# Both heads of a recurrent unit in one compact 64-wide tile: the triangular inverse, L and W by 64x64 products

## The chip, the cores and the metric

The kernel runs on one core of one Trainium2 chip. The metric is the device time of one execution in microseconds (us); before the change it is 2819.77 us, the median of 3 runs (2819.64 to 2821.25). The trace that is read here comes from one more, profiled execution.

## The reference, cut to what matters

The kernel computes two hybrid decoder layers on 512 tokens of width 1024, in f32. Each layer is a SwiGLU feed-forward, a mixer, and a second feed-forward, each with residual and layer norm. The mixer runs three token mixers beside each other on one projection of the stream and merges them: RWKV-7 (8 heads of width 64), differential attention, and a gated DeltaNet (4 heads of width 128).

RWKV-7 is a recurrence over tokens, per head:

```
S = S * w_t - (S @ kk_t) (kk_t * a_t)^T + v_t k_t^T ;   y_t = S @ r_t
```

The gated DeltaNet is given in chunks of 64 tokens. In both, the kernel works on chunks of 64 tokens. Within a chunk it needs the inverse of I + L, where L is a strictly lower triangular 64x64 matrix:

```
Lm = strict_lower(kb @ k^T * decay) ;  A = Lm + I
U = solve(A, v * beta) ;  W = solve(A, kb * exp(G))
```

512 tokens are 8 chunks, so one head has 8 such 64x64 matrices. The gated DeltaNet in this kernel uses chunks of 128 instead, so 4 matrices of 128x128.

## The kernel before

A feed-forward is a row of wide projections: for each 128 output columns, 24 matmuls of 128x128 against 512 tokens (f32 split into a high and a low f32r part, three products), with the weights streamed by SP's queue through a ring of four buffers. The mixer's projections (`proj`, PSUM tile pj or pgt) are the same, 8 blocks of 3.

The mixer's token mixers are cut into 12 units, `ORDER = RDRDRRDGGDGG`: R is `rw_pair` (one pair of RWKV heads, 4 per layer), D is `da_head`, G is `gdn_head` (4 per layer). Each unit is a Python generator; a yield ends a turn. `main` writes out the projections, and after each piece `interleave` calls `pump`, which gives turns to active units whose last results an estimate (`Estimate`) takes to be ready. At most four units are active. The instructions thus stand in one order written at build time, and the compiler's scheduler may still move independent ones against each other. All matrix work of the units goes through `mm` and `tr`, so the profile shows one line for it, L68; the PSUM tile's name tells products apart: pL, ip (all products of the inverse), pM, pMV, paT, pW, pU (the row name covers pU0 and the per-chunk pU), pb, pk.

One RWKV unit (`rw_pair`), as far as it matters:

- Before L: `be` (128 partitions = 2 heads x 64 channels, 512 tokens) is the vector b of the recurrence, and `AR` holds the a and r sides.
- L: per head and per 128 tokens, one product pL of 64x128 (contraction 64 channels) to a full 128x128 block that holds two chunks; DVE scales each of the 8 blocks by a per-token factor `n2` and by the mask `b_gt`, which is strictly lower triangular and zero between the two chunks. Each head has its own tile L of 128 x (4 blocks x 128).
- `inverse(Ls, whole)`: L goes to DRAM; its 16x16 diagonal blocks come back, one per partition, and DVE inverts them all at once in 15 steps of two operations; they go to DRAM (`Xd`, zero elsewhere) and come back as full 128x128 blocks X. DVE transposes X by 32x32 blocks to Z. Doubling from 16 to 32: per head, four 128x128 products of the masked L (`imL`) with Z, a copy by ACT, four 128x128 products with X, a subtraction and a transpose by DVE. Doubling from 32 to 64: products of 32x32, per head and per chunk position in a PSUM tile of its own (tiles ipt). For the gated DeltaNet (`whole`) one more step, of 64x64.
- Beside the inverse: pk and pb transpose `kap` and `be` to tokens on partitions. For b the second chunk of a 128-token block is wanted on the other half, so the transposes start 64 tokens early, and the first chunk takes a product of its own.
- After the inverse: pM (64x64 products in all four quadrants of the array, with both heads), pMV, then paT (transposes of a), pW, pU0, all of the last with the 128x128 blocks of Z; then eight steps over the chunks (pU, pS) and the output pY.

A matmul of two f32 operands stands in the trace as two records.

Of the kernel before, what the change touches and what calls it, by code (L numbers as in the profile page):

```python
# [9 lines left out]
F32 = mybir.dt.float32  # L10
# [37 lines left out]
BLK = 8 * (16 * 128 + 16)  # L48
# [88 lines left out]
class Net:  # L137
# [47 lines left out]
    def more_consts(self):  # L185
# [22 lines left out]
        def pair(name, src, r0):  # L208
            m = c.tile([P, P], F32, name=name)
            nc.gpsimd.tensor_copy(out=m, in_=src)  # L210
            nc.gpsimd.memset(m[r0:r0 + 64, 64 - r0:128 - r0], 0.0)
            return m

        self.b_gt = pair("b_gt", self.m_gt, 64)

        self.m3 = c.tile([P, 3, 64], F32, name="m3")
        for h in range(2):
            r = slice(64 * h, 64 * h + 64)
            for j in range(3):
# [17 lines left out]
                                fill=0.0, base=2 * b - 1, channel_multiplier=-1)  # L237
        zt = self.t2(name="zt")
        nc.gpsimd.memset(zt, 0.0)
        self.xd, self.nxd = [], 0  # L240
        for _ in range(3):
            t = self.tc.dram_tile([8 * BLK], F32, name="Xd")
            nc.sync.dma_start(out=t[0:128 * 1024].rearrange("(p c) -> p c", p=128)[:, 0:512], in_=zt)
            nc.sync.dma_start(out=t[0:128 * 1024].rearrange("(p c) -> p c", p=128)[:, 512:1024], in_=zt)
            nc.sync.dma_start(out=t[128 * 1024:].rearrange("(p c) -> p c", p=128), in_=zt[:, 0:8])
            self.xd.append(t)
# [558 lines left out]
    def inverse(self, Ls, whole):  # L805
        nc = self.nc
        n = len(Ls)
        r4 = lambda t: t.rearrange("p (n i) -> p n i", n=4)
        blk = lambda t, b: t[:, 128 * b:128 * b + 128]

        Ld = self.tc.dram_tile([8 * BLK], F32, name="Ld")
        Xd = self.xd[self.nxd % len(self.xd)]
        self.nxd += 1
        full = lambda t, e: bass.AP(t.tensor, t.offset + 4 * e * BLK, [[128, 128], [BLK, 4], [1, 128]])
        diag = lambda t: bass.AP(t.tensor, t.offset, [[BLK // 8, 32 * n], [128, 16], [1, 16]])
        B = self.t2((128, 2, 16, 16), name="LX")
        Lb, Xb = B[0:32 * n, 0], B[0:32 * n, 1]
        Tb = self.m128("Tb")[0:32 * n]
# [3 lines left out]
        for e in range(n):  # L822
            nc.sync.dma_start(out=full(Ld, e), in_=r4(Ls[e]))
        nc.sync.dma_start(out=Lb, in_=diag(Ld))
        yield
        mLs = []
        for i in range(15):
            if i % 4 == 3:
                yield
            if i == 7:  # L830
                for L in Ls:
                    mLs.append(self.t2(name="imL"))
                    nc.gpsimd.tensor_tensor(out=r4(mLs[-1]), in0=r4(L), in1=self.bc(self.lev, 4), op=ALU.mult)
            m = 15 - i
            t = Tb[:, 0:m * (i + 1)].rearrange("p (a b) -> p a b", a=m)
            nc.vector.tensor_tensor(out=t, in0=Lb[:, i + 1:16, i:i + 1].to_broadcast([32 * n, m, i + 1]),
                                    in1=Xb[:, i:i + 1, 0:i + 1].to_broadcast([32 * n, m, i + 1]), op=ALU.mult)
# [3 lines left out]
        X = [self.t2(name="iX") for _ in Ls]  # L841
        for e in range(n):
            nc.sync.dma_start(out=r4(X[e]), in_=full(Xd, e))
        yield
        Z = [self.t2(name="iZ") for _ in Ls]
        for e in range(n):
            nc.vector.transpose(out=Z[e], in_=X[e])
        for e in range(n):
# [6 lines left out]
            pz = self.psum(name="ip")  # L855
            for b in range(4):
                self.mm(blk(pz, b), blk(X[e], b), blk(mL, b), start=True, stop=True)
            nc.vector.tensor_tensor(out=Z[e], in0=Z[e], in1=pz, op=ALU.subtract)
            nc.vector.transpose(out=X[e], in_=Z[e])
            yield  # L860

        for w, at in ((32, (0, 64)),) + (((64, (0,)),) if whole else ()):
            pts = []
            for e in range(n):
                L4, Z4 = r4(Ls[e]), r4(Z[e])
                pts.append(self.t2((128, 4, w), name="ipt"))
                for a in at:
                    p = self.psum((128, 4, w), name="ip")
                    for b in range(4):
                        self.mm(p[a:a + w, b, :], L4[a + w:a + 2 * w, b, a:a + w], Z4[a + w:a + 2 * w, b, a + w:a + 2 * w],  # L870
                                start=True, stop=True)
                    nc.scalar.copy(out=pts[e][a:a + w], in_=p[a:a + w])
            yield
            for e in range(n):
                X4, Z4, pt = r4(X[e]), r4(Z[e]), pts[e]
                for a in at:
                    p = self.psum((128, 4, w), name="ip")
                    for b in range(4):
                        self.mm(p[a:a + w, b, :], X4[a:a + w, b, a:a + w], pt[a:a + w, b, :], start=True, stop=True)
                    nc.vector.tensor_scalar(out=Z4[a:a + w, :, a + w:a + 2 * w], in0=p[a:a + w], scalar1=-1.0,  # L880
                                            scalar2=None, op0=ALU.mult)
                if whole and w == 32:
                    p = self.psum((128, 4, w), name="ip")
                    for b in range(4):
                        self.mm(p[w:2 * w, b, :], pt[0:w, b, :], X4[0:w, b, 0:w], start=True, stop=True)
                    nc.scalar.activation(out=X4[w:2 * w, :, 0:w], in_=p[w:2 * w], func=ACTF.Copy, scale=-1.0)
            yield
# [33 lines left out]
    def rw_pair(self, j, r, k, v):  # L921
# [54 lines left out]
        be = t2(name="be")  # L976
        for h in range(2):
            STT(out=hv(be, h), in0=hv(ta, h), scalar=1.0, in1=AR[h][:, :, 0, :], op0=ALU.add, op1=ALU.mult)
        STT(out=be, in0=be, scalar=0.5, in1=G, op0=ALU.mult, op1=ALU.mult)
# [18 lines left out]
        Ls = [t2((128, 4, 128), name="L") for _ in range(2)]  # L998
        ps = [self.psum((128, 4, 128), "pL") for _ in range(2)]
# [9 lines left out]
        inv = self.inverse([L.rearrange("p a b -> p (a b)") for L in Ls], False)  # L1009
# [15 lines left out]
        Z = yield from inv  # L1025

        Ms, Sh = [[], []], []
        for h in range(2):
            ps = [self.psum((128, 2, 3, 64), "pM") for _ in range(2)]
            for tp in range(2):  # L1030
                for q in range(2):
# [3 lines left out]
                    for e in range(2):  # L1035
                        rs = slice(64 * e, 64 * e + 64)
                        self.mm(ps[e][qs, tp, 0:2 + q:1 + q, :], kap[rs, c], AR[h][rs, tp, :, qs], start=True, stop=True)
                        self.mm(ps[e][os, tp, 1 + q, :], be[rs, c], AR[h][rs, tp, 1, qs], start=True, stop=True)
            for e in range(2):
# [4 lines left out]
                Ms[e].append(M)  # L1044
            yield

        nb = nn2[:, :, None].to_broadcast([128, 8, 64])
        R = [t2((128, 4, 2, 64), name="R") for _ in range(2)]
        R8 = [t.rearrange("p t e i -> p (t e) i") for t in R]
# [8 lines left out]
        p = self.psum((128, 4, 128), "paT")  # L1058
        for tt in range(NT):
            self.tr(p[:, tt, :], AR[tt // 2][:, tt % 2, 0, :], self.ident)  # L1060
        TT(out=R8[1], in0=p.rearrange("p t (e i) -> p (t e) i", e=2), in1=nb, op=ALU.mult)

        p = self.psum((128, 4, 128), "pW")
        for tt in range(NT):
            for e in range(2):
                self.mm(p[64 * e:64 * e + 64, tt, :], R[1][:, tt, e, :], Z[e][:, 128 * tt:128 * tt + 128], start=True, stop=True)
        U0, W = (t.rearrange("p t e i -> p t (e i)") for t in R)
        for q in range(2):
            nc.scalar.copy(out=W[:, :, 64 - 64 * q:128 - 64 * q], in_=p[:, :, 64 * q:64 * q + 64])
        p = self.psum((128, 4, 128), "pU0")  # L1070
        for tt in range(NT):
            for e in range(2):
                for q in range(2):
                    c = 2 * tt + q
# [478 lines left out]
```

## Time and profile before

| | |
|---|---|
| median of 3 runs | 2819.77 us |
| the profiled execution | 2822.03 us |
| its span | 2820.3 us |
| mean granted TensorE clock | 0.995 |
| PE busy | 2774.4 us, 98% |
| DVE busy | 1967.5 us, 70% |
| ACT busy | 1111.8 us, 39% |
| POOL busy | 156.7 us, 6% |
| DMA | 282.21 MB, mean 100 GB/s |

The span runs from the first to the last instruction; the time of the execution has a little around it. Busy time is the union of an engine's records. Matmuls are pipelined, and their recorded ends overlap the next one's start; the distance between the starts of two records is what the first of them costs. The granted clock is 1 where TensorE runs at 2.4 GHz and 0.5 where it runs at 1.2 GHz.

The mixing stages lie at about 380 to 1000 us and 1780 to 2400 us; the rest is feed-forward.

### The profile page before, as it was taken

The numbers are of one execution on the slowest core, as the hardware profiler recorded it, in microseconds if no ns is written. First come the engines' busy times: TensorE is split into PE (matmuls) and PEld (weight loads), VectorE is DVE, ScalarE is ACT, GpSimd is POOL, SyncE is SP. The second block draws the span as 40 slices with busy tenths as digits, with TensorE's granted clock in tenths as the row PEclk, the third lists the DMA queues.
The fourth block names the chain that finished last, engine by engine and source line by source line (L and its number), as shares of the span: only waits on it lengthen the run. The fifth ranks groups of instructions, "written<-read, shape, count | busy, mean of one in ns | idle before, by whom it ended". The sixth has DMA issues, their size and how long they took to land. (4 is left out here: it accounts for less than half of the span.)

```text
span 2820.3 us, 40858 instructions
## 1 busy us (share of the span) xinstructions
PE 2774.4 (98%) x15536; PEld 2295.6 (81%) x15536; DVE 1967.5 (70%) x4400; ACT 1111.8 (39%) x2029; POOL 156.7 (6%) x205
## 2 busy tenths in 40 slices
PE   9999999999999999999999999999999999999998
PEld 7888887778888888888888888777788888888887
DVE  6766568788875466667676666677888764666675
ACT  4333345444543333333333333454445433333332
POOL 1000021010000010000100000210100000100001
PEclk9999999999999999999999999999999999999999
DMA  6233523232223353332533324223222223533322
GB/s 212 90 112 99 143 81 80 57 82 56 69 76 85 94 176 116 111 105 87 150 112 107 120 82 137 83 72 77 63 62 69 80 80 106 180 112 107 108 77 89
DMA packets 437381, 282.21 MB, mean 100 GB/s; under 512 B 40457, under 2 KB 392897, under 8 KB 437185
## 3 DMA queue, kind: packets, MB, share of 16 engines
q1 hardware_dynamic: 437184, 279.61, 33.7%
q8 instruction: 122, 2.00, 0.3%
q14 instruction: 75, 0.61, 0.1%
HBM read 258.31 MB, written 21.25 MB: 99 GB/s over the span
## 5 line engine op out<-in xcount | busy, mean ns | idle before, releaser
L68 ACT CAST wh<-wr 128x1024 fp32r<-128x1024 f32 x342 | 359.7, 1052 | 772.7 <-issue 226.1
L68 DVE TENSOR_TENSOR wl<-wr,wh 128x1024 fp32r<-128x1024 f32 x342 | 422.3, 1235 | 309.9 <-ACT wh L68 307.9
L68 PE MATMUL pu<-xTh,wh 128*128 128x512 f32 x672 | 261.6, 389 | 0.0
L68 PE MATMUL pu<-xTl,wh 128*128 128x512 f32 x672 | 261.4, 389 | 0.0
L68 PE MATMUL pu<-xTh,wl 128*128 128x512 f32 x672 | 261.4, 389 | 0.0
L68 PE MATMUL pg<-xTh,wh 128*128 128x512 f32 x640 | 249.0, 389 | 0.0
L68 PE MATMUL pg<-xTl,wh 128*128 128x512 f32 x640 | 249.0, 389 | 0.0
L68 PE MATMUL pg<-xTh,wl 128*128 128x512 f32 x640 | 249.0, 389 | 0.0
L68 DVE SCALAR_TENSOR_TENSOR x<-oa,x 128x512 f32<-128x512 f32 x320 | 212.5, 686 | 36.0 <-PE oa L68 35.6
L68 PE MATMUL pj<-xTh,wh 128*128 128x512 f32 x560 | 228.5, 408 | 0.0
L68 PE MATMUL pj<-xTh,wl 128*128 128x512 f32 x560 | 226.6, 405 | 0.0
L68 PE MATMUL pj<-xTl,wh 128*128 128x512 f32 x560 | 224.7, 401 | 0.0
L68 DVE TENSOR_TENSOR ft<-ft,pu 128x512 f32<-128x512 f32 x84 | 57.7, 687 | 172.6 <-PE pu L68 172.4
L68 PE MATMUL pgt<-xTh,wh 128*128 128x512 f32 x384 | 155.1, 404 | 0.0
L68 PE MATMUL pgt<-xTh,wl 128*128 128x512 f32 x384 | 150.7, 392 | 0.0
L68 PE MATMUL pgt<-xTl,wh 128*128 128x512 f32 x384 | 150.4, 392 | 0.0
L68 PEld LDWEIGHTS pu<-xTh,wh 128*128 128x128 f32 x672 | 126.2, 188 | 26.2
L68 PEld LDWEIGHTS pu<-xTh,wl 128*128 128x128 f32 x672 | 126.1, 188 | 26.2
L68 PEld LDWEIGHTS pu<-xTl,wh 128*128 128x128 f32 x672 | 126.2, 188 | 25.9
L68 PEld LDWEIGHTS pg<-xTh,wh 128*128 128x128 f32 x640 | 120.1, 188 | 25.0
L68 PEld LDWEIGHTS pg<-xTl,wh 128*128 128x128 f32 x640 | 120.2, 188 | 24.9
L68 PEld LDWEIGHTS pg<-xTh,wl 128*128 128x128 f32 x640 | 120.2, 188 | 24.9
(421 smaller groups left out, 6053.8 us busy)
## 6 DMA issues: line engine op xcount, KB each, us to landing
wr<-in_ffn_w_in_dram SPq DMA_DIRECT2D x176, 512.0 KB
wr<-in_mix_w_in_dram SPq DMA_DIRECT2D x132, 512.0 KB
sw<-in_ffn_w_out_dram SPq DMA_DIRECT2D x128, 256.0 KB
wr<-in_ffn_w_out_dram SPq DMA_DIRECT2D x24, 512.0 KB
wr<-in_mix_w_branch_dram SPq DMA_DIRECT2D x24, 512.0 KB
xres<-x SPq DMA_DIRECT2D x40, 256.0 KB
x<-xres SPq DMA_DIRECT2D x40, 256.0 KB
wr<-in_mix_w_out_dram SPq DMA_DIRECT2D x16, 512.0 KB
```

Of the source, the lines that this page charges most:

```text
L68: r = f(*args, **kw)
```

## The change

- L of both heads is one tile `Lc` of 128 x (2 heads x 4 x 64): chunk 2t in the upper 64 partitions, chunk 2t+1 in the lower, and no columns for the zero blocks between chunks. pL is made of 64x64 products (contraction 64), one per head and chunk, and DVE scales a head's tile with one operation. There is no mask: `b_gt` goes.
- `inverse` takes one tile: for the RWKV unit 8 blocks of 64 columns, for the gated DeltaNet 4 blocks of 128. The doubling from 16 to 32 is made of 64x64 products, block by block, the upper half of the partitions and the lower in turn, for both kinds of unit. The mask product with `lev64`, the transposes, the copy and the subtraction work once on the one tile (for the gated DeltaNet the mask product and the subtraction work on two halves). In the 32-wide step, all products of one half-step go to one PSUM tile.
- The DRAM tiles shrink to 128 x 520 elements, with two zeroed `Xd` for each kind of unit.
- `be` is stored rotated by one chunk (chunk c at position c + 1, the last chunk first), so four full transposes give the shifted layout; DVE writes it in two pieces from `b1`.
- paT and R[1] move ahead of the last part of the inverse; W is formed by 64x64 products right after the first half of pM, two PSUM tiles by chunk half; U0 has contraction 64.

```diff
     def inverse(self, L, whole):
+        n, m = (4, 128) if whole else (8, 64)
+        H = [slice(0, 64), slice(64, 128)]
+        cols = lambda q: H[q] if whole else H[0]
...
+        Z = self.t2(name="iZ")
+        L4, X4, Z4 = r(L), r(X), r(Z)
+        nc.vector.transpose(out=Z, in_=X)
+        p = self.psum((128, n, 64), name="ip")
+        for b in range(n):
+            for q in range(2):
+                self.mm(p[H[q], b, :], mL[H[q], b, :], Z4[H[q], b, cols(q)], start=True, stop=True)
+        nc.scalar.copy(out=mL, in_=p)
+        yield
+        p = self.psum((128, n, 64), name="ip")
+        for b in range(n):
+            for q in range(2):
+                self.mm(p[H[q], b, :], X4[H[q], b, cols(q)], mL[H[q], b, :], start=True, stop=True)
+        for q in range(2) if whole else range(1):
+            s = H[q] if whole else slice(0, 128)
+            nc.vector.tensor_tensor(out=Z4[s, :, cols(q)], in0=Z4[s, :, cols(q)], in1=p[s], op=ALU.subtract)
+        nc.vector.transpose(out=X, in_=Z)
+        yield
-        for e in range(n):
-            mL = mLs[e]
-            p = self.psum(name="ip")
-            for b in range(4):
-                self.mm(blk(p, b), blk(mL, b), blk(Z[e], b), start=True, stop=True)
-            nc.scalar.copy(out=mL, in_=p)
...
     def rw_pair(self, j, r, k, v):
+        bc = lambda c: slice(64 * ((c + 1) % 8), 64 * ((c + 1) % 8) + 64)
-        STT(out=be, in0=be, scalar=0.5, in1=G, op0=ALU.mult, op1=ALU.mult)
+        for a, b in ((64, 0), (0, 448)):
+            n = 64 if b else 448
+            STT(out=be[:, a:a + n], in0=b1[:, b:b + n], scalar=0.5, in1=G[:, b:b + n], op0=ALU.mult, op1=ALU.mult)
...
-                self.mm(ps[e][:, tt, :], AR[tt // 2][rs, tt % 2, 0, :], be[rs, 128 * tt:128 * tt + 128], start=True, stop=True)
+                for q in range(2):
+                    qs = slice(64 * q, 64 * q + 64)
+                    self.mm(ps[e][qs, tt, :], AR[tt // 2][rs, tt % 2, 0, qs], be[rs, bc(2 * tt + q)],
+                            start=True, stop=True)
         for e in range(2):
-            for tt in range(NT):
-                STT(out=Ls[e][:, tt, :], in0=ps[e][:, tt, :], scalar=n2[:, 2 * tt + e:2 * tt + e + 1], in1=self.b_gt,
-                    op0=ALU.mult, op1=ALU.mult)
+            TT(out=Lc[:, e], in0=ps[e], in1=n2.rearrange("p (t e) -> p e t", e=2)[:, e, :, None].to_broadcast([128, 4, 64]),
+               op=ALU.mult)
...
-        for tt in range(1, NT):
-            self.tr(p[:, tt, :], be[:, 128 * tt - 64:128 * tt + 64], self.ident)
-        self.mm(p[64:128, 0, :], be[:, 0:64], self.ident, start=True, stop=True)
+        for tt in range(NT):
+            self.tr(p[:, tt, :], be[:, 128 * tt:128 * tt + 128], self.ident)
...
+            if h == 0:
+                ps = [self.psum((128, 4, 64), "pW") for _ in range(2)]
+                for tt in range(NT):
+                    for q in range(2):
+                        qs = slice(64 * q, 64 * q + 64)
+                        for e in range(2):
+                            self.mm(ps[q][64 * e:64 * e + 64, tt, :], R[1][qs, tt, e, :], Z[qs, e, tt, :], start=True, stop=True)
-                self.mm(p[64 * e:64 * e + 64, tt, :], R[1][:, tt, e, :], Z[e][:, 128 * tt:128 * tt + 128], start=True, stop=True)
...
-                    self.mm(p[64 - 64 * q:128 - 64 * q, tt, 64 * e:64 * e + 64], Z[e][:, 64 * c:64 * c + 64], R[0][:, tt, e, :],
+                    qs = slice(64 * q, 64 * q + 64)
+                    self.mm(p[64 - 64 * q:128 - 64 * q, tt, 64 * e:64 * e + 64], Z[qs, e, tt, :], R[0][qs, tt, e, :],
                             start=True, stop=True)
```

## Rows read from the trace of the kernel before

**Rows 1.** The head of the page: span; per engine busy us, share, instructions.

```profile
span 2820.3 us, 40858 instructions
PE 2774.4 (98%) x15536; PEld 2295.6 (81%) x15536; DVE 1967.5 (70%) x4400; ACT 1111.8 (39%) x2029; POOL 156.7 (6%) x205
```

**Rows 2.** Table of stretches: stretch, length, busy us and records per engine, PEclk, DMA.

```profile
380.00:1000.00 620.00, 609.01 (x4139) 497.42 (x4138) 456.78 (x1382) 284.46 (x611) 39.95 (x53) 0.99 0.29 77
420.00:430.00 10.00, 7.96 (x34) 5.97 (x35) 6.86 (x23) 3.56 (x7) 1.76 (x2) 0.69 0.30 81
```

**Rows 3.** Timeline, PE: start, us, operation, shape, records; a doubling burst.

```profile
455.66 0.39 PE L68 MATMUL pj<-xTl,wh 128*128 128x512 f32 x1
455.89 0.39 PE L68 MATMUL pj<-xTh,wl 128*128 128x512 f32 x1
456.17 1.13 PE L68 MATMUL ip<-iZ,imL 128*128 128x128 f32 x8
457.05 0.48 PE L68 MATMUL pj<-xTh,wh 128*128 128x512 f32 x1
457.37 0.40 PE L68 MATMUL pj<-xTl,wh 128*128 128x512 f32 x1
```

**Rows 4.** Timeline, PE, 488 to 490 us: the product pMV.

```profile
488.32 0.39 PE L68 MATMUL pj<-xTh,wl 128*128 128x512 f32 x1
488.64 1.15 PE L68 MATMUL pMV<-VU,M 64*64 64x64 f32 x32
489.72 0.66 PE L68 MATMUL tk<-ident,dv 128*128 128x128 f32 x4
```

**Rows 5.** Timeline, PE, 494 to 498 us: W and U0 (named pW and pU).

```profile
494.92 1.09 PE L68 MATMUL pW<-iZ,R 128*64 128x128 f32 x16
495.84 1.10 PE L68 MATMUL pU<-R,iZ 128*64 128x64 f32 x32
496.87 0.50 PE L68 MATMUL pj<-xTl,wh 128*128 128x512 f32 x1
497.21 0.40 PE L68 MATMUL pj<-xTh,wl 128*128 128x512 f32 x1
```

**Rows 6.** Timeline, PE, 473 to 476 us: L, then a 32-wide piece.

```profile
473.50 1.16 PE L68 MATMUL pL<-be,AR 64*128 64x128 f32 x14
474.59 0.74 PE L68 MATMUL ip<-iZ,L 32*32 32x32 f32 x24
475.26 0.50 PE L68 MATMUL pj<-xTh,wh 128*128 128x512 f32 x1
```

**Rows 7.** Timeline, PE: first record of a pM burst, and what follows its 32.

```profile
649.71 0.32 PE L68 MATMUL pM<-AR,sh 64*64 64x128 f32 x1
...
650.54 0.66 PE L68 MATMUL tk<-ident,ct 128*128 128x128 f32 x4
```

**Rows 8.** Timeline, PE, 434 to 436 us: transposes of kap and of b.

```profile
434.66 0.60 PE L68 MATMUL pk<-ident,sh 128*128 128x128 f32 x4
435.09 0.85 PE L68 MATMUL pb<-ident,be 128*128 128x128 f32 x5
435.88 0.33 PE L68 MATMUL ppT<-ident,dsc 128*128 128x128 f32 x1
```

**Rows 9.** Timeline, PE, 477 to 483 us: two 32-wide pieces.

```profile
477.07 0.43 PE L68 MATMUL ip<-iZ,L 32*32 32x32 f32 x8
477.43 0.50 PE L68 MATMUL pj<-xTl,wh 128*128 128x512 f32 x1
...
481.97 0.89 PE L68 MATMUL ip<-ipt,iX 32*32 32x32 f32 x32
482.79 0.50 PE L68 MATMUL pj<-xTh,wl 128*128 128x512 f32 x1
```

**Rows 10.** Timeline, PE, 718 to 720 us: 64-wide step of a gated-delta unit.

```profile
718.58 0.68 PE L68 MATMUL ip<-iZ,gL 64*64 64x64 f32 x8
719.18 0.50 PE L68 MATMUL pj<-xTh,wh 128*128 128x512 f32 x1
```

More of the change, by code (lines that the diff above doesn't have):

```diff
@@ L47 @@
 LOADED = 1
-BLK = 8 * (16 * 128 + 16)
 WIDTH = 4
@@ L237, in more_consts @@
                                 fill=0.0, base=2 * b - 1, channel_multiplier=-1)
+        self.lev64 = c.tile([P, 64], F32, name="lev64")
+        for q in range(2):
+            nc.gpsimd.tensor_copy(out=self.lev64[64 * q:64 * q + 64, :], in_=self.lev[64 * q:64 * q + 64, 64 * q:64 * q + 64])
         zt = self.t2(name="zt")
         nc.gpsimd.memset(zt, 0.0)
[L240 to L246, printed above, removed]
+        self.xd, self.nxd = {False: [], True: []}, 0
+        for whole in (False, True, False, True):
+            t = self.tc.dram_tile([128 * 520], F32, name="Xd")
+            nc.sync.dma_start(out=t[0:128 * 512].rearrange("(p c) -> p c", p=128), in_=zt)
+            nc.sync.dma_start(out=t[128 * 512:].rearrange("(p c) -> p c", p=128), in_=zt[:, 0:8])
+            self.xd[whole].append(t)
         self.ndist = c.tile([P, 512], F32, name="ndist")
@@ L800, in params, with inverse @@
         nc.vector.tensor_scalar(out=self.nea, in0=self.nea, scalar1=-1.0, scalar2=None, op0=ALU.mult)
-    def inverse(self, Ls, whole):
+    def inverse(self, L, whole):
         nc = self.nc
[L807 to L812, printed above, removed]
-        self.nxd += 1
-        full = lambda t, e: bass.AP(t.tensor, t.offset + 4 * e * BLK, [[128, 128], [BLK, 4], [1, 128]])
-        diag = lambda t: bass.AP(t.tensor, t.offset, [[BLK // 8, 32 * n], [128, 16], [1, 16]])
+        n, m = (4, 128) if whole else (8, 64)
+        nb = 8 * n
+        r = lambda t: t.rearrange("p (n i) -> p n i", n=n)
+        H = [slice(0, 64), slice(64, 128)]
+        cols = lambda q: H[q] if whole else H[0]
+        st = 16 * m + 16
+        Ld = self.tc.dram_tile([128 * 520], F32, name="Ld")
+        xd = self.xd[whole]
+        Xd = xd[self.nxd % len(xd)]
+        self.nxd += 1
+        if whole:
+            full = lambda t, d: [(bass.AP(t.tensor, t.offset, [[m, 128], [8 * st, n], [1, m]]), r(d))]
+        else:
+            full = lambda t, d: [(bass.AP(t.tensor, t.offset + q * 4 * n * st, [[m, 64], [4 * st, n], [1, m]]), r(d)[H[q]])
+                                 for q in range(2)]
+        diag = lambda t: bass.AP(t.tensor, t.offset, [[st, nb], [m, 16], [1, 16]])
         B = self.t2((128, 2, 16, 16), name="LX")
-        Lb, Xb = B[0:32 * n, 0], B[0:32 * n, 1]
-        Tb = self.m128("Tb")[0:32 * n]
+        Lb, Xb = B[0:nb, 0], B[0:nb, 1]
+        Tb = self.m128("Tb")[0:nb]
         nc.gpsimd.memset(Xb, 1.0)
@@ L821, in inverse @@
                                 fill=0.0, base=0, channel_multiplier=0)
-        for e in range(n):
-            nc.sync.dma_start(out=full(Ld, e), in_=r4(Ls[e]))
+        for d, t in full(Ld, L):
+            nc.sync.dma_start(out=d, in_=t)
         nc.sync.dma_start(out=Lb, in_=diag(Ld))
         yield
-        mLs = []
         for i in range(15):
@@ L830, in inverse @@
             if i == 7:
[L831 to L837, printed above, removed]
+                mL = self.t2((128, n, 64), name="imL")
+                for q in range(2) if whole else range(1):
+                    s = H[q] if whole else slice(0, 128)
+                    nc.gpsimd.tensor_tensor(out=mL[s], in0=r(L)[s, :, cols(q)],
+                                            in1=self.lev64[s, None, :].to_broadcast([64 if whole else 128, n, 64]), op=ALU.mult)
+            k = 15 - i
+            t = Tb[:, 0:k * (i + 1)].rearrange("p (a b) -> p a b", a=k)
+            nc.vector.tensor_tensor(out=t, in0=Lb[:, i + 1:16, i:i + 1].to_broadcast([nb, k, i + 1]),
+                                    in1=Xb[:, i:i + 1, 0:i + 1].to_broadcast([nb, k, i + 1]), op=ALU.mult)
             nc.vector.tensor_tensor(out=Xb[:, i + 1:16, 0:i + 1], in0=Xb[:, i + 1:16, 0:i + 1], in1=t, op=ALU.subtract)
@@ L840, in inverse @@
         yield
-        X = [self.t2(name="iX") for _ in Ls]
-        for e in range(n):
-            nc.sync.dma_start(out=r4(X[e]), in_=full(Xd, e))
+        X = self.t2(name="iX")
+        for d, t in full(Xd, X):
+            nc.sync.dma_start(out=t, in_=d)
         yield
[L845 to L848, printed above, removed]
-            mL = mLs[e]
-            p = self.psum(name="ip")
-            for b in range(4):
-                self.mm(blk(p, b), blk(mL, b), blk(Z[e], b), start=True, stop=True)
-            nc.scalar.copy(out=mL, in_=p)
-            yield
[L855 to L866, printed above, removed]
-                for a in at:
[L868 to L886, printed above, removed]
@@ new lines, in inverse @@
+        for q in range(2) if whole else range(1):
+            s = H[q] if whole else slice(0, 128)
+            nc.vector.tensor_tensor(out=Z4[s, :, cols(q)], in0=Z4[s, :, cols(q)], in1=p[s], op=ALU.subtract)
+        nc.vector.transpose(out=X, in_=Z)
+        yield
+        for w, at in ((32, (0, 64)),) + (((64, (0,)),) if whole else ()):
+            c0 = lambda a: a if whole else 0
+            pt = self.t2((128, n, w), name="ipt")
+            p = self.psum((128, n, w), name="ip")
+            for b in range(n):
+                for a in at:
+                    c = c0(a)
+                    self.mm(p[a:a + w, b, :], L4[a + w:a + 2 * w, b, c:c + w], Z4[a + w:a + 2 * w, b, c + w:c + 2 * w],
+                            start=True, stop=True)
+            for a in at:
+                nc.scalar.copy(out=pt[a:a + w], in_=p[a:a + w])
+            yield
+            p = self.psum((128, n, w), name="ip")
+            for b in range(n):
+                for a in at:
+                    c = c0(a)
+                    self.mm(p[a:a + w, b, :], X4[a:a + w, b, c:c + w], pt[a:a + w, b, :], start=True, stop=True)
+            for a in at:
+                c = c0(a)
+                nc.vector.tensor_scalar(out=Z4[a:a + w, :, c + w:c + 2 * w], in0=p[a:a + w], scalar1=-1.0,
+                                        scalar2=None, op0=ALU.mult)
+            if whole and w == 32:
+                p = self.psum((128, n, w), name="ip")
+                for b in range(n):
+                    self.mm(p[w:2 * w, b, :], pt[0:w, b, :], X4[0:w, b, 0:w], start=True, stop=True)
+                nc.scalar.activation(out=X4[w:2 * w, :, 0:w], in_=p[w:2 * w], func=ACTF.Copy, scale=-1.0)
@@ L996, in rw_pair @@
         TT(out=bv, in0=v, in1=pb, op=ALU.mult)
-        Ls = [t2((128, 4, 128), name="L") for _ in range(2)]
-        ps = [self.psum((128, 4, 128), "pL") for _ in range(2)]
+        Lc = t2((128, 2, 4, 64), name="L")
+        ps = [self.psum((128, 4, 64), "pL") for _ in range(2)]
         for tt in range(NT):
@@ L1019, in rw_pair @@
         p = self.psum((128, 4, 128), "pb")
-        for tt in range(1, NT):
-            self.tr(p[:, tt, :], be[:, 128 * tt - 64:128 * tt + 64], self.ident)
-        self.mm(p[64:128, 0, :], be[:, 0:64], self.ident, start=True, stop=True)
+        for tt in range(NT):
+            self.tr(p[:, tt, :], be[:, 128 * tt:128 * tt + 128], self.ident)
         nc.scalar.copy(out=KB[0][64:128], in_=p[64:128])
         nc.scalar.copy(out=KB[1][0:64, 0:3], in_=p[0:64, 1:4])
-        Z = yield from inv
+        nb = nn2[:, :, None].to_broadcast([128, 8, 64])
+        R = [t2((128, 4, 2, 64), name="R") for _ in range(2)]
+        R8 = [t.rearrange("p t e i -> p (t e) i") for t in R]
+        U0, W = (t.rearrange("p t e i -> p t (e i)") for t in R)
+        p = self.psum((128, 4, 128), "paT")
+        for tt in range(NT):
+            self.tr(p[:, tt, :], AR[tt // 2][:, tt % 2, 0, :], self.ident)
+        TT(out=R8[1], in0=p.rearrange("p t (e i) -> p (t e) i", e=2), in1=nb, op=ALU.mult)
+        Z = (yield from inv).rearrange("p (e t i) -> p e t i", e=2, t=4)
         Ms, Sh = [[], []], []
@@ L1044, in rw_pair @@
                 Ms[e].append(M)
+            if h == 0:
+                ps = [self.psum((128, 4, 64), "pW") for _ in range(2)]
+                for tt in range(NT):
+                    for q in range(2):
+                        qs = slice(64 * q, 64 * q + 64)
+                        for e in range(2):
+                            self.mm(ps[q][64 * e:64 * e + 64, tt, :], R[1][qs, tt, e, :], Z[qs, e, tt, :], start=True, stop=True)
+                for q in range(2):
+                    nc.scalar.copy(out=W[:, :, 64 - 64 * q:128 - 64 * q], in_=ps[q])
             yield
-        nb = nn2[:, :, None].to_broadcast([128, 8, 64])
-        R = [t2((128, 4, 2, 64), name="R") for _ in range(2)]
-        R8 = [t.rearrange("p t e i -> p (t e) i") for t in R]
         p = self.psum((128, 4, 2, 64), "pMV")
@@ L1285, in gdn_head @@
         yield
-        Z, = yield from self.inverse([L.rearrange("p a b -> p (a b)")], True)
+        Z = yield from self.inverse(L.rearrange("p a b -> p (a b)"), True)
         S = None
```

26 lines of the change are left out of this document (5 added, 21 removed).

## The prediction

> **What bounds the kernel now.** I read the head of the page first. PE is busy 2774.4 us of a span of 2820.3 us, 98%; DVE, the next, has 70% [rows 1]. So PE is idle 45.9 us in all, and the kernel gets shorter mainly by what PE no longer has to do. The change touches only the two mixing stages. The table of stretches shows the first of them: between 380 and 1000 us PE is busy 609.01 us of 620, DVE 456.78, ACT 284.46 [rows 2]. Eleven microseconds of idle PE there, about 22 in both layers, are all that shorter waits can give back. DVE has room even before its load falls. A second number in that view matters: from 420 to 430 us the granted clock is 0.69 and PE is busy 7.96 us; so 0.31 x 2 x 10 = 6 us of that stretch ran at the lower level (1.2 GHz), at half speed, which costs some 3 us. PE had been idle for about 2 us of the same stretch. Of such places there are three in the two mixing stages, and I put their loss at some 8 us.
>
> Busy time is a poor price for small matmuls, because they overlap. So I price every burst in the order of time: from the start of the last wide projection matmul (pj) before it to the start of the second pj after it, less two undisturbed pj steps of 0.23 us (455.66 to 455.89) [rows 3]. One f32 matmul is two records (xN) in these rows.
>
> **Part 1, doubling of the recurrent units (inverse, both products).** Before, each head has two bursts of four full 128x128 products, eight records each. In the row, pj starts at 455.89, the burst at 456.17, the next pj at 457.05 and the one after it at 457.37: 1.48 us less 0.46, that is 1.02 us, of which 0.88 is the burst itself [rows 3]. I take 0.95, between these two, since a burst next to other 128x128 work pays no entry or exit. Four bursts per unit: 3.8 us. After, both heads lie in one tile, and each product is 8 blocks x 2 halves = 16 products of 64x64, 32 records, where half q reads partitions of half q and writes PSUM partitions of half q. The trace has just this shape: pMV, 32 records of 64*64, alternating the same two quadrants, into one PSUM tile. It takes 1.08 us (488.64 to 489.72), and the entry from pj costs 0.32 instead of 0.23 [rows 4]. The exit costs again: after the tiled burst of pU the next pj takes 0.34 (496.87 to 497.21) instead of 0.23 [rows 5]. So 1.08 + 0.09 + 0.11 = 1.28 us, twice per unit: 2.56. Gain 1.24 us a unit, with 8 units (4 pairs of heads x 2 layers) 9.9 us. With both of the old burst prices: 0.96 to 1.52 a unit, 8 to 12 us.
>
> **Part 2, the same step of the gated-delta units** (eight of them; they call the same function with 4 blocks of 128). Before two full bursts, 1.9 us. After two bursts of 16 records; half of pMV's 1.08 is 0.54, and I add 0.06 for the drain that a short burst spreads over fewer records, and the 0.20 of entry and exit: 0.80. Gain 0.3 x 8 = 2.4 us (bounds 1.3 and 3.9, from 0.88 and 1.02 before and 0.80 and 0.78 after).
>
> **Part 3, L.** Before 16 records of 64*128; 14 of them take 1.09 us, exit drain included (473.50 to 474.59) [rows 6]; 16 make some 1.2. After 32 records of 64*64 in all four quadrants, as pM does it: 32 records, some twice as wide, in 0.83 us (649.71 to 650.54) [rows 7]. Both are tiled and pay the same at entry and exit. Gain 0.35 x 8 = 2.8 us; bounds 0 (issue sets the pace) and 4.
>
> **Part 4, b's transposes.** Before, three transposes and one 128x64 product, 5 records with a change of tiling in the middle: 435.09 to 435.88, 0.79 us. After, four plain transposes: pk just ahead takes 0.43 (434.66 to 435.09) [rows 8]. 0.36 and a little for the exit that is gone: 0.4 x 8 = 3.2 us (2.9 to 4). The rotated b costs DVE one more short operation per unit, on an engine that has over 150 us of room per layer [rows 2].
>
> **Part 5, the 32-wide step.** The count of products is unchanged (64 records a unit), but now each product is one burst into one PSUM tile instead of four tiles that ACT or DVE must empty. Before, it is cut up: 24 records in 0.67 us (474.59 to 475.26) and 8 in 0.36 (477.07 to 477.43), against 32 in one piece in 0.82 (481.97 to 482.79) [rows 6, 9]. A cut thus costs 0.21, and 0.20 more for one more entry and exit. Of such pieces I count 14 in a layer's 256 records (3 of 24, 5 of 8, 4 of 16, one each of 32 and 48), where 8 would do: 6 cuts x 0.41 x 2 layers = 4.9 us. Some cuts will stay: I take 4 (0 to 5).
>
> **Part 6, W and U0.** Before 0.09 + 0.92 (494.92 to 495.84) + 1.03 (to 496.87) + 0.11 = 2.15 us [rows 5]. After, W is 32 four-quadrant records (0.83 as pM) and U0 32 records in two quadrants (1.08 as pMV), with one or two more pairs of entry and exit: 2.1 to 2.3. Taken as 0 (-1 to +1 in all). The transposes for W and R[1] only move, ahead of the inverse's end. W now waits for Z and R[1] in front of the second half of pM and the pj's behind it; Z is out before the unit goes on at all, and R[1] needs one DVE operation after paT, a turn or more earlier, so I price this wait at 0, and at the 5 us below if it is not covered.
>
> **What is not on PE.** Per unit DVE loses six of eight scalings of L, two of four 32x32-block transposes and one of two subtractions, POOL one of two mask products, ACT the smaller copies; the gated-delta units pay one more DVE and one more POOL operation. All of it lies beside PE; where PE waits now for one of these, it waits less. Against that, the units have two turns fewer, so all later turns fall at other places among the pj's. I take 0 for waits and allow a gain of 6 and a loss of 5. On SP's queue the DMAs of the inverse keep their number (L out, diagonal in, diagonal out, X back in); rows of 256 bytes replace rows of 512. The weight loads queue behind them as before, and no PE wait of the mixing stage is large enough to carry them: 11 us in all [rows 2].
>
> **Sum.** 9.9 + 2.4 + 2.8 + 3.2 + 4 + 0 = 22.3 us on PE, with nothing of it hidden, since PE sets the pace. Some new 64x64 bursts will be cut by a pj between, at 0.41 each: 16 doubling bursts, and as many L and W; six cuts are 2.4. That leaves 20 us. The profiled execution took 2822.0 us (1.7 around its span), the median of the runs shown is 2819.8; from the median I forecast 2800 us.
>
> **Rivals.**
> (a) The two halves don't run beside each other. The doubling and U0 after the change send two row halves of the array into one PSUM tile. If these took turns, each 64x64 product would cost what a lone quadrant costs: 8 records in 0.60 us (718.58 to 719.18) [rows 10], some 0.064 a record, so 2.1 + 0.2 = 2.3 us for 32. Doubling then costs 4.6 against 3.8 (+0.8), U0 2.3 against 1.1 (+1.2), the gated-delta step 2 x 1.25 against 1.9 (+0.6): 2.6 x 8 = +21, less parts 3 to 5 (10.0), +11: 2831 us, slower. It decides as soon as the pace is over 0.05 a record. Against it: pMV does the same into one tile at 0.034 a record [rows 4]. The Trainium skill, page TensorEngine Tiling (Array Packing), section "Restrictions and Gotchas" (Gotcha 1), says that different row tiles cannot access the same PSUM bank at the same time; by that rule this rival would be the forecast, and this case's trace, with pMV's 1.08 us for 32 records, does not agree.
> (b) The moved turns cost what they save. If idle PE and half-clock stretches grow by half of what they are now in the two layers (22 us of idle, some 8 us lost to the clock), 15 of the 20 us are gone: 2815. For it: an idle stretch of 2 us stands where 3 us more are lost to the clock [rows 2]. Against it: DVE, the busiest engine beside PE [rows 2], gets less to do (L's eight operations become two, transposes and subtraction are halved).
> (c) The waits shorten as well, and nothing is cut: 22 plus 6 of the 22 us of idle: 2792.
>
> **Chances.** Forecast (2795 to 2807) 0.55; (c) 0.15; (b), with a smaller loss between 2807 and 2818, 0.22; no change or a little slower by the same path 0.04; (a) 0.04. The range 2786 to 2814 leaves out (a) and the worse part of (b). A difference under 0.2%, 5.6 us, can't be told from no change. Faster by more: below 2814.1, 0.88; within: 0.05; slower: 0.07.
>
> **What would show it.** Right: the profile after has ip records of 64*64 in bursts of 32 lasting about 1.1 us, and no 128*128 ip; five records of pb become four; PE's busy time falls by about 20 us and its share stays near 98%. Wrong: 64x64 bursts of 2 us (rival a); a PE idle sum well over 46 us or a mean clock under 0.99 (rival b); a count of 64x64 pieces much above 32 in a layer, which would mean that the cuts eat part 1.

## The result, and the profile after

| | before | after |
|---|---|---|
| median of 4 runs, us | 2819.7 (2818.42 to 2821.25) | 2786.97 (2782.88 to 2789.64) |
| span of the profiled execution | 2820.3 | 2784.0 |
| PE busy | 2774.4 | 2741.7 |
| PE idle (span less busy) | 45.9 | 42.3 |
| mean granted clock | 0.995 | 0.997 |

The ratio is 0.9879, 95% interval 0.9865 to 0.9893: faster by 33 us, where 20 were forecast. On the 2819.8 us of the forecast the ratio gives 2785.7, just under the range. The changed kernel's page begins so (span; per engine busy us, share, instructions), beside [rows 1]:

```profile
span 2784.0 us, 41955 instructions
PE 2741.7 (98%) x16168; PEld 2264.7 (81%) x16168; DVE 1931.2 (69%) x4328; ACT 1101.8 (40%) x2005; POOL 150.2 (5%) x205
```

PE bounds it as before, with 98%. The span fell by 36.3 us: 32.7 of PE's busy time and 3.6 of idle. Part of the busy time is work at half speed. (1 - clock) x span bounds what that can cost: 14.1 us before, 8.4 after, so at most 5.7 of the 32.7 (the clock is given to 0.001, which is 2.8 us of the span).

In the table of stretches (length, then busy us and records of PE, PEld, DVE, ACT, POOL, clock, DMA), beside [rows 2]:

```profile
380.00:1000.00 620.00, 610.17 (x4508) 495.10 (x4508) 446.44 (x1354) 284.33 (x605) 36.34 (x53) 0.99 0.29 77
420.00:430.00 10.00, 9.89 (x54) 7.40 (x55) 4.50 (x10) 2.82 (x6) 1.29 (x1) 0.52 0.33 73
```

DVE lost 10 us in the stage, as it should. From 420 to 430 us PE is busy almost throughout, and the clock is at its lower level nearly all the time: here the changed kernel is worse off than before.

The timeline of PE (start, us, operation, shape, records), beside [rows 3, 6, 8, 9]:

```profile
432.50 0.60 PE L67 MATMUL pk<-ident,sh 128*128 128x128 f32 x4
432.94 0.60 PE L67 MATMUL pb<-ident,be 128*128 128x128 f32 x4
433.37 0.60 PE L67 MATMUL paT<-ident,AR 128*128 128x128 f32 x4
...
455.44 0.39 PE L67 MATMUL pj<-xTl,wh 128*128 128x512 f32 x1
455.76 1.15 PE L67 MATMUL ip<-iZ,imL 64*64 64x64 f32 x32
456.83 0.50 PE L67 MATMUL pj<-xTh,wl 128*128 128x512 f32 x1
457.17 0.39 PE L67 MATMUL pj<-xTh,wh 128*128 128x512 f32 x1
...
462.16 0.69 PE L67 MATMUL ip<-iZ,L 32*32 32x32 f32 x32
462.78 0.55 PE L67 MATMUL ppT<-ident,dsc 128*128 128x128 f32 x3
...
475.90 0.57 PE L67 MATMUL pL<-be,AR 64*64 64x64 f32 x22
476.40 0.51 PE L67 MATMUL pb<-sql,r_bd 128*128 128x512 f32 x1
...
576.58 0.44 PE L67 MATMUL pL<-be,AR 64*64 64x64 f32 x10
576.95 0.49 PE L67 MATMUL pS<-VU,KB 128*128 128x128 f32 x2
```

- Doubling: 32 records of 64*64 take 1.07 us (455.76 to 456.83), the entry 0.32 and the exit 0.34, to the digit what pMV and pU had shown.
- b: four transposes take 0.43 (432.94 to 433.37), where the five records took 0.79.
- L, mostly cut by a pb: a piece of 22 records takes 0.50 (475.90 to 476.40), one of 10 takes 0.37 (576.58 to 576.95), together 0.87. Before, two pieces of 8 took 0.64 each.
- The 32-wide step: 32 records of 32*32 in 0.62 (462.16 to 462.78). The same number took 0.82 before [rows 9]. This was not forecast.

The tile's own rows (minimum, median, maximum ns; first and last start; forms) show no 128*128 record left in the inverse:

```profile
L67 PE MATMUL ip<-iZ,imL x384: 218/218/267, 455.8 to 2239.2; 64*64 64x64 f32 x192
L67 PE MATMUL ip<-iZ,L x256: 191/191/212, 462.2 to 1997.8; 32*32 32x32 f32 x128
```

I summed over the whole trace, for each PSUM tile, the distances from one record's start to the next one's, less idle (before to after, us): ip 78.2 to 54.5, pj 417.4 to 409.7, pL 13.3 to 7.5, pb 13.7 to 10.2, pW 7.4 to 7.0. All other tiles together rose by 8.4, which leaves PE's 32.7. pj, whose matmuls are the same, carries entries, exits and half-speed stretches, and so do the others. Of ip's 23.7 us, the doubling gave 15.1 (48 bursts of 0.88 became 16 of 1.08 and 16 of 0.61) and the 32-wide step the other 8.6: 6.2 in the recurrent units and 2.4 in the gated-delta units.

### The profile page after: what moved, and what is told of

It is laid out like the page before. It is cut to its first block, busy times and chain, and to the rows that moved or that the text cites. A ratio compares the mean times of both kernels' runs of the same rounds, so it can differ in the third digit from the quotient of the medians.

```text
span 2784.0 us, 41955 instructions
## 1 busy us (share of the span) xinstructions
PE 2741.7 (98%) x16168; PEld 2264.7 (81%) x16168; DVE 1931.2 (69%) x4328; ACT 1101.8 (40%) x2005; POOL 150.2 (5%) x205
```

## The experiments

The gain is 13 us larger than forecast, and two things in the traces are off: the pace of the 32-wide step, and PE's waits with the clock, which I had put at nothing. Theory: the exchanged loops, which put neighbouring products into two quadrants in turn, made the step faster. Rival: it is only that it is cut into fewer pieces. For the rest, theory: less work on DVE shortened the waits. Rival: the turns fell well in this order and would fall otherwise in another. All times below are medians; ratios are to the kernel before, run on the same chip.

**The changed kernel again.** No edit: how far the result repeats.

> The changed kernel once more, as the base for the runs beside it: 2787 us, within 2783 to 2790. Every theory says the same.

Measured 2784.49 us, 0.9874 [0.986, 0.9887]. The place where the clock falls differs from run to run. This run:

```profile
420.00:430.00 10.00, 9.77 (x82) 7.98 (x83) 6.75 (x21) 5.72 (x14) 1.29 (x1) 1.00 0.54 128
1800.00:1812.00 12.00, 10.29 (x65) 7.95 (x66) 6.53 (x21) 4.02 (x7) 1.28 (x1) 0.72 0.30 66
```

In the first profile 1800 to 1812 us had clock 1.00 and 420 to 430 had 0.52. A half-speed stretch at one place of one profile thus need not be a property of the kernel.

**32-wide step, one quadrant after the other.** Theory: the step got faster because its products now alternate between two quadrants; rival: because it is in fewer pieces.

```diff
-            for b in range(n):
-                for a in at:
+            for a in at:
+                for b in range(n):
...
```

(The same in the second half-step.)

> The changed kernel, with the 32-wide step's two loops swapped: all blocks of one quadrant, then all of the other, still into one PSUM tile and in one piece. Theory (turns of quadrants): a burst of 32 records goes back from 0.62 us to about 1.0 (some 0.029 us a record, as it was before the change), 16 bursts x 0.38 = 6 us, and the gated-delta bursts lose 0.15 us x 16 = 2.4: +8.5 us over the changed kernel, about 2795. Rival (fewer pieces and fewer PSUM tiles made the step cheaper, as I had priced it): no change, 2787. Rival (moved waits and the clock made the surplus): no change either.

Measured 2791.85 us, 0.9898 [0.9884, 0.9912]: 7.4 us over the run above. The timeline:

```profile
510.49 1.09 PE L67 MATMUL ip<-iZ,L 32*32 32x32 f32 x32
511.51 0.49 PE L67 MATMUL pU<-S,R 128*128 128x128 f32 x2
```

The same 32 records in one piece take 1.02 us (510.49 to 511.51) and not 0.62; ip's sum rose by 9.2 us. One piece without the turns is thus no faster than the step was before. But the edit overshoots: it keeps one quadrant for 16 records, where the kernel before changed it every 8, and there a piece of 32 took 0.82 us [rows 9]. What the turns and the pieces are worth apart stands at "The turns alone" below.

**Doubling, one half after the other.** The same exchange of loops (`for q` outside `for b`) in both doubling products.

> The changed kernel, with the doubling's products of the upper half all ahead of those of the lower half. Theory (turns of quadrants): a 32-record burst goes from 1.08 us to about 2.1, a 16-record burst from 0.61 to 1.1: 16 x 1.0 + 16 x 0.5 = +24 us, about 2811. Rival (the 64x64 form is cheap by itself, whatever the order): 2787.

Measured 2802.25 us, 0.9933 [0.9919, 0.9946].

```profile
457.19 1.90 PE L67 MATMUL ip<-iZ,imL 64*64 64x64 f32 x32
459.02 0.50 PE L67 MATMUL pj<-xTh,wl 128*128 128x512 f32 x1
```

1.83 us (457.19 to 459.02) against 1.07, with the same products. ip's sum rose by 16.3 us, the time by 17.8; two thirds to three quarters of the 24 that I expected, but the same sign and place. The bursts follow each other on PE in the order of the changed kernel throughout, so no turn moved. Without the alternation parts 1 and 2 would be lost.

**L, two quadrants after two.** Heads outermost, so that two quadrants alternate and not four.

> The changed kernel, with L's products ordered by head, so that only two quadrants of the array take turns instead of four. Theory (turns of quadrants): L's 32 records go from about 0.65 us to pMV's 1.08, +0.4 x 8 = 3 us, about 2790. Rival (the issue of records sets L's pace): no change, 2787.

The 22-record pieces went from 0.50 to 0.67 us, the 10-record ones from 0.37 to 0.49. The time, 2785.37 (0.9877 [0.9864, 0.9891]), can't be told from the changed kernel's: seen in the trace, too small for the times.

**The turns alone, in the kernel before.**

```diff
...
+                ps = [self.psum((128, 4, w), name="ip") for _ in at]
                 for b in range(4):
+                    for a, p in zip(at, ps):
...
```

> The kernel before with one thing changed: in the 32-wide step the two quadrants of a head take turns, block by block, each still into its own PSUM tile. Theory (turns of quadrants): the step's bursts go from 26.4 us in all to about 18, -7 to -9 us, 2811 to 2813. Rival (pieces and PSUM tiles): four tiles and their pieces are still there, so no change, 2819.7.

Missed: 2823.12 us, 1.0002 [0.9992, 1.0011]. Pieces of 16 went from 0.52 to 0.37 us and ip's sum fell by 4.6, but idle time rose from 45.9 to 49.7 us. A piece of 16 in the kernel before, then in this one:

```profile
578.78 0.59 PE L68 MATMUL ip<-iZ,L 32*32 32x32 f32 x16
579.30 0.50 PE L68 MATMUL pj<-xTl,wh 128*128 128x512 f32 x1
```

```profile
580.32 0.44 PE L68 MATMUL ip<-iZ,L 32*32 32x32 f32 x16
580.69 0.50 PE L68 MATMUL pj<-xTh,wl 128*128 128x512 f32 x1
```

Summed as above, the bursts of the 32-wide step, in us, with the number of pieces:

| | recurrent units | gated-delta units |
|---|---|---|
| before | 16.5 (28) | 9.9 (18) |
| before, turns alone | 14.0 (30) | 7.2 (16) |
| after | 10.3 (18) | 7.5 (18) |
| after, one quadrant after the other | 16.4 (16) | 10.1 (20) |

So the turns alone take 5.2 us off the step, from 26.4 to 21.2 and not to 18, about equally in both kinds of unit. The other 3.7 in the recurrent units come with the fewer pieces; the gated-delta units gained nothing more. Both theory and rival of the 32-wide step are true in part.

The table of waits (us in total, times, longest) has, for this run and then for the kernel before,

```profile
PE ip L68 <- DVE iZ L68: 5.4, 4, 1.5
PE pW L68 <- DVE R L68: 1.5, 2, 0.7
```

```profile
PE ip L68 <- DVE iZ L68: 3.7, 4, 1.4
```

and no wait of pW for R. Most of what the bursts gained in the profiled execution was spent waiting: 3.8 us more of idle, 3.2 of it in these two. The order of the bursts moved as well.

**Rotated b alone, in the kernel before.** L's products then read two runs of 64 columns in place of one of 128.

```diff
-                self.mm(ps[e][:, tt, :], AR[tt // 2][rs, tt % 2, 0, :], be[rs, 128 * tt:128 * tt + 128], ...
+                for q in range(2):
+                    self.mm(ps[e][:, tt, 64 * q:64 * q + 64], AR[tt // 2][rs, tt % 2, 0, :], be[rs, bc(2 * tt + q)], ...
```

> The kernel before with the rotated b alone (four plain transposes; L by products half as wide and twice as many, in the same two row halves). Theory: the 128x64 product and its change of tiling go, -0.4 us a unit, -3.2 us; L at no change; 2816.5. Rival (the extra L records cost what the transposes save): 2819.7.

Missed, above both: 2831.93 us, 1.0037 [1.0024, 1.0049]. pb fell by the 3.6 us that part 4 says, pL rose by 7.0, and the clock's mean fell to 0.991, though the order of the bursts is almost the same. The 3.4 us more of pL and pb are a third of the loss; the half-speed bound rose from 14.1 to 25.5. The timelines of the experiment and of the kernel before:

```profile
586.33 1.77 PE L68 MATMUL pL<-be,AR 64*128 64x64 f32 x26
588.03 0.50 PE L68 MATMUL pb<-sql,r_bd 128*128 128x512 f32 x1
```

```profile
586.48 0.71 PE L68 MATMUL pL<-be,AR 64*128 64x128 f32 x8
587.12 0.49 PE L68 MATMUL pb<-sql,r_bd 128*128 128x512 f32 x1
```

26 records of 64*128 with 64 columns to stream take 1.70 us, 65 ns each; 8 with 128 columns 0.64, 80 ns each. Two records of 64 columns thus cost 1.6 times one of 128. So b's rotation alone loses here; in the change it comes with L's own products cut to 64x64, where L gets cheaper.

**Doubling by 64x64 alone, in the kernel before** (heads in separate tiles).

> The kernel before with the doubling by 64x64 products, but each head in its own tile with zero blocks, as before. Theory (form and compact tile both count): a recurrent unit has four bursts of 16 records, 0.61 + 0.2 us, instead of 0.88 + 0.07: -4.4 us, the gated-delta units -2.2; together -6.6, 2813; the rest of the change's -12 needs both heads in one burst. Rival (the form alone does it): -12, 2808. Rival (more copies and subtractions cost waits): 2817 to 2822.

Missed, and by much: 2846.08 us, 1.0087 [1.0073, 1.0101]. Waits and one of two equal stretches:

```profile
PE ip L68 <- DVE iZ L68: 12.4, 11, 3.7
PE pyT L68 <- DVE gO L68: 7.6, 4, 3.1
```

```profile
740.00:775.00 35.00, 28.22 (x181) 23.15 (x180) 21.71 (x67) 14.33 (x43) 0.80 (x2) 0.71 0.27 69
```

ip's sum fell by only 3.1 us, idle time rose by 15, and PE ran 58% of these 35 us at half speed (0.29 x 2). The doubling's own bursts did fall, from 42.1 to 33.1 us; the 32-wide and 64-wide steps, which the edit does not touch, rose by 5.9, with the half speed and with more pieces. So the form pays on PE by itself, and the rest was lost beside it. This is rival (b), in another kernel.

**A wait of 2.1 us for gg, twice.** gg holds scalars of the gated-delta units, which DVE makes. Their turns were put off, to see if the wait goes.

```diff
-            it[2] = self.est.stage
+            it[2] = self.est.stage + (LATER if it[0] == 3 else 0.0)     # LATER = 3000.0
```

> The changed kernel, with the turns of the gated-delta scalars (pG) put off by 3 us of planned PE time, so that PE needn't wait 2.1 us for them in each layer, after which the clock fell. Theory (that wait brings the half clock): two waits of 2.1 us and one or two stretches of half clock go, 4 + 3 to 8 us: 2776 to 2780. Rival (the clock falls there for another reason, or another wait comes up instead): 2783 to 2787.

Inconclusive: 2786.08 us (0.9877 [0.9862, 0.9892]), and the wait is still there, 4.3 us in two: the bursts stand in the same order as without the edit, so it did not move what it was meant to move. The kernel before has the same wait (4.1 us in two), so it explains no difference.

**DVE's old work put back**, as operations whose results nothing reads (two transposes and a subtraction per unit, six scalings of L).

> The changed kernel with the DVE work that the change took away put back as idle duties: per recurrent unit two more 32x32-block transposes, one more subtraction of a whole tile and six more scalings, all into scratch tiles that nothing reads; some 4 us of DVE a unit, 35 us in all. Theory (the compact tile also shortened PE's waits, by giving DVE less to do in the chain): idle PE and half-clock stretches grow, +4 to +10 us, 2789 to 2795. Rival (DVE lies beside PE, as I had forecast): 2785, with PE's idle sum unchanged at 33 us.

Missed, by theory and rival: 2821.32 us, 1.0002 [0.9992, 1.0011], the whole gain gone, with idle 64.5 us (42.3 in the changed kernel, by the same measure, and not the 33 of the text above), clock 0.990. Yet DVE's busy time, 1953.0 us, is still below the kernel before's. The load or the order? See the runs on CAP.

**Gated-delta doubling by full 128x128 products again**, the rest as changed.

> The changed kernel with the gated-delta units' doubling by full 128x128 products as before, the recurrent units as changed. Theory (price in the order of time): bursts of 0.61 + 0.2 us become 0.88 + 0.07 again, 16 x 0.14 = +2.2 us, 2787.5. Rival (small products in a unit with one head's tile cost waits, as they did in the kernel before): 2780 or less, faster without them.

2791.89 us, 0.9896 [0.9877, 0.9914]: 5 us above the first run of the changed kernel, 7 above the second; ip's sum rose by 3.9 and idle by 4.4, but PE's busy time in all by only 0.4. That points to a gain from part 2 and doesn't contradict its 2.4 us; more than that this run doesn't tell, since the intervals of the two ratios overlap and idle time is most of the loss in the profiled execution.

**L ahead of pb, and the update of X in turn with the other products.**

> The changed kernel with L's products written ahead of the product pb, so that L is one burst of 32 records instead of two with a change of tiling between; and with the gated-delta units' third 32-wide product (for X) in turn with the other two. Theory (a cut costs a drain and an entry and exit): 8 x 0.35 = -3 us and 8 x 0.1 = -1 us: 2781. Rival (pb's waits then stand elsewhere, or the two weren't apart for order's sake): 2785.

Missed: 2814.52 us, 0.9977 [0.9968, 0.9987], with 60.5 us of idle and clock 0.991.

```profile
PE ip L67 <- DVE iZ L67: 9.8, 7, 2.9
PE pj L67 <- DVE dq L67: 4.7, 2, 2.4
PE pL L67 <- DVE be L67: 3.2, 4, 1.1
```

L now waits for `be` at once, a projection for `dq`, and the inverse waits 9.8 us for iZ, where the changed kernel waits 1.5. Two things were edited here together, and the order of the bursts moved with them.

**W behind pMV, as before the change.**

> The changed kernel with W's products behind pMV, directly before U0, as they stood before the change; still by 64x64 products. Theory (W costs nothing either way): it then stands next to U0, which is tiled alike, instead of next to pM: 2785, within 1.5. Rival (W early is part of the surplus, because it fills a wait): 2788 to 2790.

2786.09 us, 0.9874 [0.9856, 0.9893]. W's place costs nothing that the times can tell.

**The same versions in another order.** The question left was whether the last losses come from the edits or from the places at which the turns fall. CAP is how much of the units' estimated work `interleave` lets in after each piece of the projections; it moves turns and changes no product.

```diff
-CAP = 1300.0
+CAP = 1200.0
```

(1400.0 in the last two.)

> The kernel before with CAP 1200 instead of 1300: the same operations, other turns. Theory (order decides idle and clock by tens of us, PE's work stays): PE busy less half-clock loss stays at 2760 within 5, time anywhere from 2815 to 2845. Rival (idle belongs to the operations): 2820 within 5.

> The changed kernel with CAP 1200. Theory (order): PE busy less half-clock loss stays at 2733 within 5, time anywhere from 2780 to 2815. Rival (idle belongs to the operations): 2786 within 5.

> The version with L ahead of pb, with CAP 1200. Theory (its 28 us were the order's): about 2780 to 2800, with an idle sum near 45. Rival (L first makes PE wait for b, whatever the order): 2810 or more, with waits of pL for be again.

> The version with the old DVE load put back as idle duties, with CAP 1200. Theory (order): below 2805. Rival (the units' chains can't carry the DVE work that the compact tile took away): 2815 or more, an idle sum of 60 us again.

> The kernel before with CAP 1400. Theory (order): PE busy less half-clock loss at 2760 within 5, time from 2815 to 2845. Rival (idle belongs to the operations): 2820 within 5.

> The changed kernel with CAP 1400. Theory (order): PE busy less half-clock loss at 2733 within 5, time from 2780 to 2815. Rival (idle belongs to the operations): 2786 within 5.

| CAP | before | after | difference | of PE busy | of idle | half-speed bound, before and after |
|---|---|---|---|---|---|---|
| 1200 | 2861.6 | 2813.8 | 47.8 | 39.7 | 8.9 | 28.6, 11.2 |
| 1300 | 2819.7 | 2787.0 | 32.7 | 32.7 | 3.6 | 14.1, 8.4 |
| 1400 | 2820.6 | 2789.3 | 31.3 | 29.6 | 0.9 | 8.5, 8.4 |

The differences in PE busy and idle are those of the profiled executions. The cleanest pair is CAP 1400, where clock (0.997) and idle time are alike; the kernel before, then the changed one:

```profile
span 2817.5 us, 40854 instructions
PE 2771.3 (98%) x15536; PEld 2292.5 (81%) x15536; DVE 1959.6 (70%) x4400; ACT 1111.1 (39%) x2029; POOL 158.7 (6%) x205
```

```profile
span 2787.0 us, 41963 instructions
PE 2741.7 (98%) x16168; PEld 2263.0 (81%) x16168; DVE 1926.5 (69%) x4328; ACT 1102.3 (40%) x2005; POOL 149.0 (5%) x205
```

At equal clock PE's work fell by 29.6 us. PE busy less the half-speed bound came to 2762, 2760 and 2763 us before (at 1200, 1300, 1400) and to 2740, 2733 and 2733 after. So the theory holds within its 5 us but for the changed kernel at 1200, 7 over; and the time of the kernel before at 1200 lies above the 2845 that it allowed. A constant that changes no product costs the kernel before 42 us and the changed one 27 at 1200: as much as the change is worth. With DVE's old work put back, CAP 1200 takes 2798.09 us (0.9914 [0.9899, 0.9929]), 23 below the same version at 1300 and 16 below the changed kernel at 1200. So the loss of some 35 us at 1300 is no price of DVE's load as such: in another order the same load costs nothing. L first takes 2831.82 (1.0033 [1.002, 1.0046]), as its rival said: still 18 above the changed kernel at the same CAP, with the waits for `be` (3.8 us) and `dq` (4.7) again. How much of its loss is the edit's own and how much the order's was not separated.

## Why the forecast was too small

- **The bound was read rightly.** PE kept 98%, and the time fell with PE's busy time, nothing hidden.
- **Parts 1 and 2** (12.3 us): that was 15.4 for the bursts alone, less some 3 for entries and exits. The bursts gave 15.1, and the new ones pay the 0.32 and 0.34 beside pj that were taken. **Part 3** (2.8): 0.41 a unit by the pieces shown, 4.7 by pL's sums at CAP 1400. The prediction took L before as one burst of some 1.2 us; pb cut it in two in every unit, and it cost 1.5. **Part 4** (3.2): 3.5. **Part 6** (0): pW 0.4 less, U0 0.4 more, and no change when W was moved back. W's wait for Z, priced at 0, came to 1.7 us in two.
- **Part 5 is the step that failed**, in its size and in its reach. It said that "the count of products is unchanged", priced each burst at its old pace and took only the recurrent units' cuts as gain: 4 us. But the loops were exchanged with the tiles, in both kinds of unit: blocks outside, quadrants inside (the description of the change does not say so). In a piece of 32 a record fell from 26 ns (0.82 / 32) to 19 (0.62 / 32). The step's bursts fell by 8.6 us: 6.2 in the recurrent units and 2.4 in the gated-delta units, whose 32-wide step stands in no part of the sum. The turns, put at nothing, are about 5 of the 8.6 by the run with the turns alone; the other 3.7 are the fewer pieces. The pieces of a layer fell from 14 to 9, 5 x 0.20 x 2 = 2.0 more if each entry and exit costs what the prediction took: 10.6. So the cuts, at 3.7 + 2.0, were priced not far off, and the turns were missing. I had the rows: pMV, two quadrants in turn, against the lone quadrant of the 64-wide step [rows 4, 10], and used them for part 1 and rival (a) alone. The experiments with the loops exchanged, after and before, show it.
- **The cuts** (2.4 off): none of the 32 doubling bursts was cut. L is cut by pb in all eight units, as it was before, and W in two.
- With these, 9.9 + 2.4 + 4.7 + 3.5 + 10.6 = 31.1 us, beside 29.6 measured at equal clock. The entries and exits in this sum are prices of the prediction. By the tiles' sums at CAP 1400, without any price: ip 23.4, pL 4.7, pb 3.4 and pW 0.7 less, 32.2 together; pj 6.3 less and all other tiles 8.9 more, which is 29.6. Which neighbour pays which entry was not separated.
- **Waits and clock** (0, +6 to -5): idle time gave 3.6 us at this order, which with the 29.6 makes 33; the clock gave at most 5.7 of the profiled pair. The sign was luck: the bounds were far too narrow for a term that CAP alone moves by 27 to 42 us.
- **Rivals.** (a) falls: 1.07 us a burst and not 2.1. It would have been nearer, at 1.83, had the halves not been in turn. (b) did not happen here, but waits and clock ate the gain of the turns alone and of the doubling alone, and of two versions of the changed kernel: its mechanism is real. (c), 2792, was nearest in time, for another reason in its larger part.

What is not settled: why a given order brings these half-speed stretches and waits. The waits name the late operand (iZ, be, dq), not what put it late.

## What to carry to other kernels

When small matmuls are regrouped, price the order of the loops and not only their count: neighbours in different quadrants overlap, neighbours in one don't. Check for each loop that the diff exchanges which quadrant follows which. And where an order is laid out at build time, compare two versions at several settings of its free constant before a few tens of us are put down to an edit; an edit tried alone can lose in waits what it gains in work.

## What the runs showed of the hardware

- 32x32 records, 32 in a piece: 19 ns each with two quadrants in turn product by product (0.62 us), 26 with the quadrant changed every 8 records (0.82), 32 with 16 records in one quadrant and then 16 in the other (1.02). 64x64: 33 ns in turn (1.07 us), 57 apart (1.83).
- Two row halves that write one PSUM tile in turn do overlap: 32 records take 1.07 us in turn and 1.83 us with one half after the other. By the Trainium skill, page TensorEngine Tiling (Array Packing), section "Restrictions and Gotchas" (Gotcha 1), different row tiles cannot access one PSUM bank at once; a rule that made the halves take turns would leave nothing to gain from their order, so the two times don't agree with it, and the measurement decides.
- With 64 rows of contraction and 128 output partitions, 64 streamed columns cost 65 ns a record and 128 columns 80.
- The stretch in which the clock falls to 1.2 GHz differs between two runs of one kernel (420 to 430 us: 0.52 and 1.00, PE busy 9.89 and 9.77 us of 10 there).
